# Two plain column tiles instead of four, and five groups instead of four, in the second FFN of a hybrid encoder block

## The chip, the cores and the metric

The kernel runs on one core of one Trainium2 chip. The metric is the device time of one execution in microseconds (us); lower is better. TensorE is called PE in the rows of the profile, its weight loads PEld, VectorE DVE, ScalarE ACT, GpSimd POOL, and SP is the engine that issues most DMAs.

## The reference

The block adds three things in turn to a hidden state h of 528 tokens (16 learned meta tokens and 512 real ones) by 1024 features, all in float32:

```python
h = h + 0.5 * swiglu(rms_norm(h, ffn1_norm), ffn1_w_gate, ffn1_w_up, ffn1_w_down)
u = rms_norm(h, mix_norm)
z = u @ w_in            # HGRN2 (bidirectional gated recurrence) and axial GQA from slices of z
h = h + mixed @ w_out   # mixed: both branches, gated
h = h + 0.5 * swiglu(rms_norm(h, ffn2_norm), ffn2_w_gate, ffn2_w_up, ffn2_w_down)
return h[:, N_META:]

def swiglu(x, w_gate, w_up, w_down):
    return (silu(x @ w_gate) * (x @ w_up)) @ w_down
```

The width of both FFNs is 2816, which is 22 column tiles of 128.

## The kernel before

Everything is held with features on the 128 partitions and tokens along the free dimension. The hidden state h is eight tiles of 128 x 528. The first FFN works on all 528 tokens, the second on the 512 real ones.

**Split operands.** A float32 product is made of three matmuls of a narrower type: each operand is split into a high part (a cast on ScalarE, line 84 for weights) and the rest (a subtraction on DVE, line 85), and high x high, high x rest and rest x high are summed in PSUM. `Weights` reads a list of blocks (the plan): for each block a DMA from SP into one of two `raw` buffers, then the split into `whi` and `wlo` (two buffers each); at most two blocks are prepared ahead of the one in use.

**Plain column tiles.** For the first four column tiles of an FFN (`GROUPS` and `PLAIN`), gate and up are each one `group`: 8 blocks of the contraction x 3 matmuls of 512 columns (in the first FFN 256 and 272). The normalisation's gain is folded into the operand `xt` (buffers `xh`, `xl`), and its factor R = 1/rms is applied to the results: DVE multiplies gate and up by R, ScalarE applies silu, DVE multiplies both, and the hidden tile is split into `hh` and `hl` (lines 449, 450, 452, 453, 272 and 273).

**Pairs of column tiles.** The other 18 column tiles are taken two at a time, with seven products of half size instead of eight (Winograd's form of Strassen's scheme). Contraction, tokens and columns are each cut in two; sums and differences of the four quarters of the input are multiplied by sums and differences of the four quarters of the weights. `pair` runs, for gate and for up, the products P1 (input part b11), P2 (b21), P5 (n1), P6 (n2), P7 (t3), P3 (b22) and P4 (t4), each of 4 x 3 matmuls of 256 columns (264 in the first FFN), 14 products in all. Weight sums are made by `Weights.seven` on DVE and GpSimd, and are split like other blocks: two "first", two "sums", two "more", one "last" block for a pair, in that order.

**Input parts.** `normal` prepares the input parts. `early(kk)`, for each of four kk, normalises two tiles of h into `xn` (line 331), makes n1 and n2 in `xm` (lines 335 to 337) and splits b11, b21, n1 and n2. The plain loop calls it once behind each of the four column tiles. `late()`, behind the plain tiles, makes t3, b22 and t4 (lines 351 to 353) and splits them. Its results lie in the same buffers `xh` and `xl` that the plain products read as `xt`:

```python
room = [sp.tile([P, 4, 4, nh], F32R, name=m, tag=m) for m in ("xh", "xl")]
for i, nm in enumerate(("t3", "b22", "t4")):
    parts_of[nm] = tuple(r[:, i] for r in room)
```

`xm` has a single buffer, in `early` and in `late`.

**Groups.** Behind the column tiles of each group (4, 6, 6 and 6 of them) stand the products with W_down: for each of the eight feature tiles c one weight block of 128 x (128 x group size) and 3 matmuls of 512 columns for each hidden tile; DVE then adds half of the result to h (line 468). Behind the last group's addition the second FFN stores the tile; the last feature tile is done in two halves.

**Order.** Outside the mixing stage in the middle (whose matmuls are in an order written out in the program) the instructions of an engine are ordered by a planner, by their place in the program and by when their operands are expected; the engines wait for each other through semaphores.

Of the kernel before, what the change touches and what calls it, by code (L numbers as in the profile page):

```python
# [11 lines left out]
ALU = mybir.AluOpType  # L12
# [6 lines left out]
SEQ = 512  # L19
META = 16  # L20
T = SEQ + META
# [3 lines left out]
CUT = 256  # L25
DFF = 2816
NF = DFF // P
GROUPS = ((0, 4), (4, 10), (10, 16), (16, 22))
PLAIN = 4
HEADS = 4  # L30
OFFSET = 300
EARLY = 7
# [8 lines left out]
C_FFN1, C_MIX, C_FFN2, C_LBF, C_LBB, C_ON = 0, 8, 16, 24, 32, 40  # L41
# [142 lines left out]
def block_kernel(tc, xT, wg1, wu1, wd1, w_in, wup, wout, wg2, wu2, wd2, params,  # L184
                 cosT, sinT, masks, ident_in, out):
    nc = tc.nc
    act, dve, pe, pool = nc.scalar, nc.vector, nc.tensor, nc.gpsimd

    def group(outs, w, xs, tick=None):
        hi, lo = w  # L190
        n = len(xs)
        for k in range(n):
            sl = slice(k * P, (k + 1) * P)
            xh, xl = xs[k]
            for i, (a, b) in enumerate(((hi, xh), (hi, xl), (lo, xh))):
                for o, cols in outs:
                    pe.matmul(o, a[:, sl], b[:, cols], start=(k == 0 and i == 0),  # L197
                              stop=(k == n - 1 and i == 2))
            if tick:
                tick(0.65 if len(outs) == 1 else 0.68)  # L200

    with (tc.tile_pool(name="persist", bufs=1) as sp, tc.tile_pool(name="wts", bufs=1) as wp,
          tc.tile_pool(name="psum", bufs=1, space=PSUM) as pp):
        W = Weights(nc, wp, 2)

        def ffn_plan(wg, wu, wd):
            plan = []
            for a, b in GROUPS:
                if b <= PLAIN:
                    for j in range(a, b):  # L210
                        plan += [wg[j], wu[j]]
                else:
                    for j in range(a, b, 2):
                        plan += W.seven([wg[j], wg[j + 1], wu[j], wu[j + 1]])
                plan += [wd[c][:, a * P:b * P] for c in range(KT)]
            return plan
# [32 lines left out]
        def parts(n):  # L249

            nonlocal turn
            turn += 1
            if n == SEQ:
                return [(bank(("mm", "mm", "mm", "at", "am")[turn % 5]), slice(0, SEQ))]
            if turn % 3 == 0:
                t = wide("S")
                return [(t[:, 512 - CUT:512], FULL[0]), (t[:, 512:512 + T - CUT], FULL[1])]
            return [(bank(g)[:, :c.stop - c.start], c) for g, c in zip((("mm", "mm"), ("at", "am"))[turn % 3 - 1], FULL)]
# [12 lines left out]
        def split(dst, src, cols=slice(0, T)):  # L271
            act.copy(dst[0][:, cols], src[:, cols])
            dve.tensor_tensor(dst[1][:, cols], src[:, cols], dst[0][:, cols].bitcast(F32), ALU.subtract)
# [32 lines left out]
        def normal(ft, xt, gain, n):  # L306


            nh = n // 2
            E, F = slice(0, nh), slice(nh, n)  # L310
            xn = ft.tile([P, KT, n], F32, name="xn", tag="xn")
            parts_of = {}

            def new(name, pool_t, tags):
                parts_of[name] = tuple(pool_t(t) for t in tags)

            def unit(t):
                return ft.tile([P, 4, nh], F32R, name=t, tag=t)

            def both(name, kk, src):  # L320
                hi, lo = (t[:, kk, :] for t in parts_of[name])
                act.copy(hi, src)
                dve.tensor_tensor(lo, src, hi.bitcast(F32), ALU.subtract)

            def early(kk):

                if not kk:
                    for nm in ("b11", "b21", "n1", "n2"):
                        new(nm, unit, (nm + "h", nm + "l"))
                for k in (kk, kk + 4):  # L330
                    dve.scalar_tensor_tensor(xn[:, k], h[k][:, :n], par[:, gain + k:gain + k + 1], R[:, :n],
                                             ALU.mult, ALU.mult)
                u, v = xn[:, kk], xn[:, kk + 4]
                t = ft.tile([P, 2, nh], F32, name="xm", tag="xm", bufs=1)
                dve.tensor_tensor(t[:, 0], u[:, E], u[:, F], ALU.subtract)
                dve.tensor_tensor(t[:, 1], t[:, 0], v[:, F], ALU.add)
                dve.tensor_scalar(t[:, 1], t[:, 1], -1.0, None, ALU.mult)
                both("b11", kk, u[:, E])
                both("b21", kk, v[:, E])
                both("n1", kk, t[:, 0])  # L340
                both("n2", kk, t[:, 1])

            def late():
# [4 lines that stand above are left out]
                for kk in range(4):  # L348
                    u, v = xn[:, kk], xn[:, kk + 4]
                    t = ft.tile([P, 2, nh], F32, name="xm", tag="xm", bufs=1)  # L350
                    dve.tensor_tensor(t[:, 0], v[:, F], u[:, F], ALU.subtract)
                    dve.tensor_tensor(t[:, 1], t[:, 0], u[:, E], ALU.add)
                    dve.tensor_tensor(t[:, 1], t[:, 1], v[:, E], ALU.subtract)
                    both("t3", kk, t[:, 0])
                    both("b22", kk, v[:, F])
                    both("t4", kk, t[:, 1])

            return parts_of, early, late

        def pair(ft, xq, n):  # L360
# [69 lines left out]
                step(i, w, i, "P4")  # L430
            return tiles[1]

        def ffn(ft, xt, gain, n, last):
            def hidden(u):
                hh, hl = (ft.tile([P, TP if n == T else SEQ], F32R, name=m, tag=m, bufs=7)[:, :n] for m in ("hh", "hl"))
                split((hh, hl), u, slice(0, n))
                return hh, hl

            xq, early, late = normal(ft, xt, gain, n)
            for a, b in GROUPS:  # L440
                h1 = []
                for j in range(a, b) if b <= PLAIN else ():
                    pg = parts(n)
                    group(pg, W.next(), xt)
                    pu = parts(n)
                    group(pu, W.next(), xt)
                    g, u = (ft.tile([P, TP], F32, name=t, tag=t, bufs=3)[:, :T] for t in ("g", "u"))
                    for o, c in pg:
                        dve.tensor_tensor(g[:, c], o, R[:, c], ALU.mult)
                    act.activation(g[:, :n], g[:, :n], AF.Silu)  # L450
                    for o, c in pu:
                        dve.tensor_tensor(u[:, c], o, R[:, c], ALU.mult)
                    dve.tensor_tensor(u[:, :n], u[:, :n], g[:, :n], ALU.mult)
                    h1.append(hidden(u))
                    early(j)
                if b <= PLAIN:
                    late()
                for j in range(a, b, 2) if b > PLAIN else ():
                    for u in pair(ft, xq, n):
                        h1.append(hidden(u))  # L460
                for c in range(KT):
                    w = W.next()
                    ends = b == NF and n == SEQ and c == KT - 1
                    for po in ([[(bank(g)[:, :256], slice(i, i + 256))] for g, i in (("at", 0), ("am", 256))]
                               if ends else [parts(n)]):
                        group(po, w, h1)
                        for o, cols in po:
                            dve.scalar_tensor_tensor(h[c][:, cols], o, 0.5, h[c][:, cols], ALU.mult, ALU.add)  # L468
                        if ends:
                            last(c, po[0][1])  # L470
                    if b == NF and not ends:
                        last(c)

        with tc.tile_pool(name="f1", bufs=1) as ft:
            xt = xtiles()
            W.extra = ft
            plan = ffn_plan(wg1, wu1, wd1)
            plan.insert(14, masks)
            W.plan(plan)
            dummy = ft.tile([P, 32], F32, name="dummy", tag="dummy")  # L480
# [15 lines left out]
            for k in range(KT):  # L496
                a = sums[k % 2]
# [20 lines left out]
            plan = [w_in[c] for c in order]  # L518
# [2 lines left out]
            for c in range(KT):  # L521
                plan += [w_in[Z_GA + c], wup[c][:, :512]]
            plan += [wout[c] for c in range(KT)]
            W.plan(plan + ffn_plan(wg2, wu2, wd2))
            ffn(ft, xt, C_FFN1, T, last1)


        with tc.tile_pool(name="mix", bufs=1) as mp, tc.manual_schedule(engines={pe.engine}):
# [54 lines left out]
            with tc.tile_pool(name="heads", bufs=1) as hp, tc.tile_pool(name="small", bufs=1) as mn:  # L583
# [415 lines left out]
                for c in range(KT):  # L999
# [3 lines left out]
                    b = branch(YB)  # L1003
# [5 lines left out]
            with tc.tile_pool(name="tail", bufs=1) as hp:  # L1009
# [10 lines left out]
                for c in range(KT):  # L1020
                    sg = tmp()[:, :SEQ]
                    gate(sg)
                    b = branch(YA)
# [3 lines left out]
                xt2 = xtiles(SEQ)  # L1027
                for c in range(KT):
                    b = bank("mm")
# [6 lines left out]
        with tc.tile_pool(name="f2", bufs=1) as ft:  # L1036
            W.extra = ft

            def last2(c, cols=slice(0, SEQ)):
                nc.sync.dma_start(out=out[c * P:(c + 1) * P, cols], in_=h[c][:, cols])  # L1040

            ffn(ft, xt2, C_FFN2, SEQ, last2)


def _constants():
# [59 lines left out]
```

## Time and profile before

| | |
|---|---|
| Median of 3 runs | 1206.66 us (1203.74 to 1207.83) |
| The profiled execution | 1206.21 us |
| Its span, first to last instruction | 1204.4 us |
| Mean granted clock of TensorE | 0.991 |
| Busy: PE, PEld, DVE, ACT, POOL | 1172.3, 1074.0, 879.4, 554.2, 195.2 us |

The span is cut from one execution; times in the rows count from its start. Matmuls are pipelined, so that a busy PE isn't one at its peak; weight loads run beside them. Busy times of neighbouring instructions on an engine overlap a little.

### The profile page before, as it was taken

How to read it: one execution, taken by the hardware profiler on the slowest of the kernel's cores; microseconds unless marked ns; L12 is line 12 of the kernel's file. 1: busy time of each engine (PE TensorE's matmuls, PEld its weight loads, DVE VectorE, ACT ScalarE, POOL GpSimd, SP SyncE). 2: the span in 40 equal slices, each digit the busy share in tenths (PEclk: the TensorE clock that was granted, in tenths of full speed). 3: DMA queues.
4: the chain of work that ended last, by engine and by line, in shares of the span. 5: the costliest groups of instructions: out<-in, count | busy, mean ns of one | idle time of the engine just before them, and what ended most of it. 6: DMA issues, size and time to landing. Idle time of an engine off the chain costs nothing.

```text
span 1204.4 us, 19449 instructions
## 1 busy us (share of the span) xinstructions
PE 1172.3 (97%) x7765; PEld 1074.0 (89%) x7765; DVE 879.4 (73%) x1440; ACT 554.2 (46%) x920; POOL 195.2 (16%) x158
## 2 busy tenths in 40 slices
PE   8999999999999998989999999999999999999998
PEld 8999999999999787868888788888888998998997
DVE  7988758848956788798698845454788856866863
ACT  5545425524545464545336533334444533543541
POOL 1012001001102023242132410122101101101100
PEclk9999999999999998999899999999999999999999
DMA  6133223232223210101011112233423332333213
GB/s 232 63 104 132 88 88 106 97 97 96 72 66 120 74 68 35 54 28 60 36 54 36 54 53 103 91 105 105 142 68 110 114 101 97 106 101 103 95 53 122
DMA packets 34234, 106.22 MB, mean 88 GB/s; under 512 B 3936, under 2 KB 4320, under 8 KB 34144
## 3 DMA queue, kind: packets, MB, share of 16 engines
q1 hardware_dynamic: 33984, 104.44, 26.0%
q8 instruction: 61, 1.00, 0.3%
q0 software_dynamic: 160, 0.54, 0.1%
q14 instruction: 29, 0.24, 0.1%
HBM read 102.87 MB, written 2.10 MB: 87 GB/s over the span
## 4 chain that ended last, share of the span: by engine, by line
PE 85%; DVE 10%; issue 2%; ACT 2%; DMA 0%; POOL 0%; SPq 0%; ACTq 0%; DVEq 0%; POOLq 0%
PE mm L197 34%; PE mm L374 14%; PE at L374 9%; PE at L197 5%; PE am L197 5%; PE gs L374 4%; PE S L197 4%; PE am L374 2%; PE gs L884 2%; DVE wlo L85 2%; PE mm L938 1%; PE mm L732 1%; PE S L694 1%; PE at L717 1%; ACT whi L84 1%
## 5 line engine op out<-in xcount | busy, mean ns | idle before, releaser
L84 ACT CAST whi<-raw 128x1024 fp32r<-128x1024 f32 (+2 forms) x220 | 189.5, 862 | 286.6 <-PE mm L197 123.8
L85 DVE TENSOR_TENSOR wlo<-raw,whi 128x1024 fp32r<-128x1024 f32 (+2 forms) x220 | 223.5, 1018 | 24.9 <-ACT whi L84 20.1
L197 PE MATMUL mm<-xh,whi 128*128 128x512 f32 (+1 forms) x504 | 166.8, 364 | 9.9 <-DVE tm L543 2.3
L197 PE MATMUL mm<-xl,whi 128*128 128x512 f32 (+1 forms) x504 | 160.0, 351 | 0.4 <-DVE xl L279 0.3
L197 PE MATMUL mm<-xh,wlo 128*128 128x512 f32 (+1 forms) x504 | 159.2, 349 | 0.3 <-DVE wlo L85 0.3
L116 POOL TENSOR_TENSOR sums<-raw 128x512 f32<-128x512 f32 x36 | 59.0, 1639 | 492.4 <-DVE wlo L85 492.4
L197 PEld LDWEIGHTS mm<-xh,whi 128*128 128x128 f32 x504 | 89.8, 191 | 23.2 <-DVE tm L543 2.7
L85 DVE TENSOR_TENSOR wlo<-sums,whi 128x1024 fp32r<-128x1024 f32 x72 | 87.6, 1218 | 24.9 <-ACT whi L84 24.7
L84 ACT CAST whi<-sums 128x1024 fp32r<-128x1024 f32 x72 | 75.4, 1051 | 62.6 <-DVE sums L111 21.0
L197 PEld LDWEIGHTS mm<-xh,wlo 128*128 128x128 f32 x504 | 89.1, 190 | 13.4 <-DVE wlo L85 0.8
L197 PEld LDWEIGHTS mm<-xl,whi 128*128 128x128 f32 x504 | 89.8, 192 | 10.4 <-DVE xl L279 0.9
L871 POOL TENSOR_TENSOR Z<-Z,tot 128x512 f32<-128x512 f32 x32 | 48.0, 1499 | 154.4 <-PE gs L884 129.3
L197 PE MATMUL mm<-hh,whi 128*128 128x256 f32 (+1 forms) x218 | 62.9, 333 | 0.1
L197 PE MATMUL mm<-hh,wlo 128*128 128x256 f32 (+1 forms) x218 | 63.0, 334 | 0.0
L197 PE MATMUL mm<-hl,whi 128*128 128x256 f32 (+1 forms) x218 | 62.9, 332 | 0.0
L374 PE MATMUL mm<-xl,whi 128*128 128x264 f32 (+1 forms) x216 | 61.3, 284 | 0.0
L374 PE MATMUL mm<-xh,whi 128*128 128x264 f32 (+1 forms) x216 | 61.2, 283 | 0.0
L374 PE MATMUL mm<-xh,wlo 128*128 128x264 f32 (+1 forms) x216 | 61.2, 283 | 0.0
L468 DVE SCALAR_TENSOR_TENSOR h<-mm,h 128x512 f32<-128x512 f32 (+2 forms) x40 | 21.0, 545 | 41.5 <-PE mm L197 41.3
L702 ACT ACTIVATE pr<-S,nm,yq 128x528 f32<-128x528 f32 x32 | 25.4, 794 | 38.0 <-DVE nm L699 33.7
L884 PE MATMUL gs<-Z,ks 128*128 128x128 f32 x224 | 33.7, 296 | 9.0 <-DVE A L888 3.6
L884 PEld LDWEIGHTS gs<-Z,ks 128*128 128x128 f32 x224 | 30.6, 198 | 12.8 <-issue 7.3
(367 smaller groups left out, 3418.4 us busy)
## 6 DMA issues: line engine op xcount, KB each, us to landing
raw<-in_wg SPq DMA_DIRECT2D x43, 512.0 KB, 3.3
raw<-in_wu SPq DMA_DIRECT2D x43, 512.0 KB, 3.2
raw<-in_w_in SPq DMA_DIRECT2D x42, 512.0 KB, 3.2
raw<-in_wd SPq DMA_DIRECT2D x48, 384.0 KB, 3.1
raw<-in_wd SPq DMA_DIRECT2D x16, 256.0 KB, 2.6
raw<-in_wup SPq DMA_DIRECT2D x16, 256.0 KB, 2.6
raw<-in_wout SPq DMA_DIRECT2D x8, 512.0 KB, 3.3
h<-in_xT SPq DMA_DIRECT2D x4, 528.0 KB, 6.5
```

Of the source, the lines that this page charges most:

```text
L84: nc.scalar.copy(hi[:, c], src)
L85: nc.vector.tensor_tensor(lo[:, c], src, hi[:, c].bitcast(F32), ALU.subtract)
L116: nc.gpsimd.tensor_tensor(t[:, E], r0[:, E], r1[:, E], ALU.add)
L197: pe.matmul(o, a[:, sl], b[:, cols], start=(k == 0 and i == 0), stop=(k == n - 1 and i == 2))
L374: pe.matmul(o, a[:, sl], b[:, kk, :], start=(start and kk == 0 and i == 0), stop=(kk == 3 and i == 2), skip_group_check=True)
L468: dve.scalar_tensor_tensor(h[c][:, cols], o, 0.5, h[c][:, cols], ALU.mult, ALU.add)
L694: pe.matmul(s[:, WIDE][:, cols], st[e][:, c * P:(c + 1) * P], kk[:, cols], start=(i == 0), stop=(i == 1))
L702: act.activation(pr, s[:, WIDE], AF.Exp, bias=nm, scale=r, accum_out=sm)
L717: pe.transpose(o[:, k, :], pr[:, k * P:(k + 1) * P], ident)
L732: pe.matmul(av, v[:, k, :], p[:, k, :], start=(k == 0 and i == 0), stop=False)
L871: pool.tensor_tensor(xx, xx, first, ALU.mult)
L884: pe.matmul(s[:, c, :], ks[:, c * P:(c + 1) * P], ap(Z, T + c * P, ((2 * m, P // (2 * m)), (T + m, 2), (1, m))), start=True, stop=True)
```

## The change

The second FFN gets groups of its own: 2, 6, 6, 4 and 4 column tiles, of which the first two are plain, so that ten pairs stand where nine stood and two plain tiles where four stood. The first FFN keeps 4, 6, 6 and 6. With two plain tiles, `early` is called twice behind each. In both FFNs, n2 is made by one scalar_tensor_tensor, behind the split of n1, instead of a tensor_tensor and a tensor_scalar.

```diff
-GROUPS = ((0, 4), (4, 10), (10, 16), (16, 22))
-PLAIN = 4
+GROUPS1 = ((0, 4), (4, 10), (10, 16), (16, 22))
+GROUPS2 = ((0, 2), (2, 8), (8, 14), (14, 18), (18, 22))
...
-        def ffn_plan(wg, wu, wd):
+        def ffn_plan(wg, wu, wd, groups):
             plan = []
-            for a, b in GROUPS:
-                if b <= PLAIN:
+            for a, b in groups:
+                if not a:
                     for j in range(a, b):
                         plan += [wg[j], wu[j]]
...
                 dve.tensor_tensor(t[:, 0], u[:, E], u[:, F], ALU.subtract)
-                dve.tensor_tensor(t[:, 1], t[:, 0], v[:, F], ALU.add)
-                dve.tensor_scalar(t[:, 1], t[:, 1], -1.0, None, ALU.mult)
                 both("b11", kk, u[:, E])
                 both("b21", kk, v[:, E])
                 both("n1", kk, t[:, 0])
+                dve.scalar_tensor_tensor(t[:, 1], t[:, 0], -1.0, v[:, F], ALU.mult, ALU.subtract)
                 both("n2", kk, t[:, 1])
...
-            for a, b in GROUPS:
+            for a, b in groups:
                 h1 = []
-                for j in range(a, b) if b <= PLAIN else ():
+                for j in () if a else range(b):
...
-                    early(j)
-                if b <= PLAIN:
+                    for kk in range(4 * j // b, 4 * (j + 1) // b):
+                        early(kk)
+                if not a:
                     late()
-                for j in range(a, b, 2) if b > PLAIN else ():
+                for j in range(a, b, 2) if a else ():
...
-            plan = ffn_plan(wg1, wu1, wd1)
+            plan = ffn_plan(wg1, wu1, wd1, GROUPS1)
...
-            W.plan(plan + ffn_plan(wg2, wu2, wd2))
-            ffn(ft, xt, C_FFN1, T, last1)
+            W.plan(plan + ffn_plan(wg2, wu2, wd2, GROUPS2))
+            ffn(ft, xt, C_FFN1, T, GROUPS1, last1)
...
-            ffn(ft, xt2, C_FFN2, SEQ, last2)
+            ffn(ft, xt2, C_FFN2, SEQ, GROUPS2, last2)
```

## Rows read from the trace of the kernel before

**Rows 1.** The page: the chain that ended last, by engine.

```profile
PE 85%; DVE 10%; issue 2%; ACT 2%; DMA 0%; POOL 0%; SPq 0%; ACTq 0%; DVEq 0%; POOLq 0%
```

**Rows 2.** Stretches of the second FFN: busy us (instructions), granted clock, DMA share, GB/s.

```profile
core 0: us, PE busy (x) PEld busy (x) DVE busy (x) ACT busy (x) POOL busy (x), PEclk, DMA share, GB/s
852.17:896.88 44.71, 44.71 (x196) 36.51 (x195) 38.33 (x66) 20.83 (x36) 0.00 (x0) 1.00 0.33 112
896.88:922.96 26.08, 25.90 (x122) 20.60 (x121) 23.44 (x44) 12.23 (x24) 1.30 (x1) 1.00 0.30 91
922.96:943.30 20.34, 20.34 (x168) 20.24 (x169) 18.66 (x27) 12.43 (x21) 3.72 (x3) 1.00 0.38 131
...
1013.50:1074.40 60.90, 60.90 (x505) 60.62 (x505) 51.52 (x72) 33.74 (x56) 9.20 (x5) 1.00 0.33 106
...
1168.00:1204.40 36.40, 33.04 (x162) 27.65 (x161) 12.41 (x18) 5.67 (x7) 0.00 (x0) 0.99 0.35 113
```

**Rows 3.** TensorE's timeline in the second FFN: start us, duration us, instruction.

```profile
874.95 0.39 PE L197 MATMUL mm<-xh,whi 128*128 128x512 f32 x1
...
896.71 0.39 PE L197 MATMUL am<-hh,whi 128*128 128x512 f32 x1
...
919.61 0.28 PE L374 MATMUL mm<-b11h,whi 128*128 128x256 f32 x1
```

**Rows 4.** The chain in order of time: start us, us, matmuls and their count.

```profile
864.23 5.44 PE at L197 x24
...
1016.37 1.66 PE at L374 x12
...
1022.35 1.44 PE gs L374 x12
...
1086.67 4.08 PE at L197 x18
```

**Rows 5.** DVE's timeline in the second FFN; in brackets idle us before, and releaser.

```profile
862.05 0.68 DVE L449 TENSOR_TENSOR g<-mm,R 128x512 f32<-128x512 f32 x1
862.64 1.41 DVE L331 SCALAR_TENSOR_TENSOR xn<-h,par,R 128x512 f32<-128x512 f32 x2
863.97 0.42 DVE L335 TENSOR_TENSOR xm<-xn 128x256 f32<-128x256 f32 x1
...
865.84 1.22 DVE L85 TENSOR_TENSOR wlo<-raw,whi 128x1024 fp32r<-128x1024 f32 x1
866.98 0.68 DVE L273 TENSOR_TENSOR hl<-u,hh 128x512 fp32r<-128x512 f32 x1
867.58 0.28 DVE L337 TENSOR_SCALAR xm<-xm 128x256 f32<-128x256 f32 x1
867.78 0.42 DVE L323 TENSOR_TENSOR b11l<-xn,b11h 128x256 fp32r<-128x256 f32 x1
868.12 0.42 DVE L323 TENSOR_TENSOR b21l<-xn,b21h 128x256 fp32r<-128x256 f32 x1
...
896.91 0.69 DVE L452 TENSOR_TENSOR u<-at,R 128x512 f32<-128x512 f32 x1 [3.85 <-PE at L197]
...
903.97 0.69 DVE L468 SCALAR_TENSOR_TENSOR h<-am,h 128x512 f32<-128x512 f32 x1
...
910.00 0.43 DVE L323 TENSOR_TENSOR xl<-xm,xh 128x256 fp32r<-128x256 f32 x1 [0.26 <-ACT xh L322]
```

**Rows 6.** DVE's timeline in the first pair of the second FFN.

```profile
936.92 0.42 DVE L397 SCALAR_TENSOR_TENSOR u<-u,g 128x256 f32<-128x256 f32 x1
```

**Rows 7.** The page, DMA issues: engine, count, KB each, median us to landing.

```profile
raw<-in_wd SPq DMA_DIRECT2D x16, 256.0 KB, 2.6
```

**Rows 8.** TensorE's timeline in the mixing stage; in brackets idle us before.

```profile
573.14 1.22 PE L938 MATMUL mm<-vt,A 128*128 128x128 f32 x4 [3.08 <-DVE st L927]
```

**Rows 9.** A stretch of the mixing stage, TensorE alone: busy us, clock, DMA share, GB/s.

```profile
570.00:580.00 10.00, 6.92 (x37) 0.66 0.00 0
```

**Rows 10.** A stretch of the first FFN, behind its plain tiles, TensorE alone.

```profile
65.00:70.00 5.00, 4.68 (x37) 1.00 0.20 56
```

**Rows 11.** DVE's timeline at the end of the last pair.

```profile
1169.19 0.69 DVE L273 TENSOR_TENSOR hl<-u,hh 128x512 fp32r<-128x512 f32 x1 [0.69 <-ACT hh L272]
```

More of the change, by code (lines that the diff above doesn't have):

```diff
@@ L431, in pair, with ffn @@
             return tiles[1]
-        def ffn(ft, xt, gain, n, last):
+        def ffn(ft, xt, gain, n, groups, last):
             def hidden(u):
```

## The prediction

> **What bounds the kernel now.** I read the page first: the chain that ended last is TensorE for 85% and VectorE (DVE) for 10% [rows 1], so as a whole the matmuls bind. The second FFN is then cut into stretches [rows 2]. TensorE is busy from end to end in each but the tail; DVE fills 38.33 of the 44.71 us of the plain tiles, 23.44 of the 26.08 us behind them and 18.66 of the first pair's 20.34 us. So DVE is nearly a second bound in just the stretch that the change shortens.
>
> TensorE's timeline gives the dates [rows 3]: the plain tiles start at 852.17 (where the first stretch of rows 2 is cut), the third of them at 874.95, the products with W_down at 896.71, the first pair's product P1 (b11) at 919.61 us. The chain in order of time gives prices [rows 4]: 24 plain matmuls of 512 columns take 5.44 us (227 ns each), 12 of a pair's 256 columns 1.44 us (120 ns), 18 of the down products 4.08 us (227 ns). The 96 down matmuls of the first group should take 96 x 0.227 = 21.8 us; from 896.71 to 919.61 are 22.9, so only 1.1 us are lost there today.
>
> DVE's timeline says why so little [rows 5]. With R ready, DVE is free at 862.05 and works without a break up to a wait of 3.85 us, which the last plain product ends at 896.91. late() can't be finished before that: its tiles t3, b22, t4 lie in the buffers xh and xl that the plain products read. So it runs behind the plain tiles, under 21.8 us of down products.
>
> **The change part by part.** *TensorE.* Two plain tiles go: 4 x 5.44 = 21.8 us. One pair comes: three pairs took 60.90 us [rows 2], 20.3 each. Saved: 1.5 us. The down products stay 22 x 3 x 8 matmuls in all.
>
> By the Trainium skill (TensorE: Matmul & The Clock Gate, Back-to-back issue gap) a sustained stream spaces 512-column matmuls 131 ns apart and 128-column ones 81; an estimate between them for 256 columns is 98 ns, so two plain tiles would take 96 x 131 ns = 12.6 us and a pair 168 x 98 ns = 16.4 us, and the sum below would be 5.3 us higher. The trace disagrees: 227 and 120 ns [rows 4].
>
> *DVE at the transition.* I price an instruction by the distance to the next start in a run without idle time, since neighbours overlap [rows 5]: 0.60 us for a 512-column tensor_tensor or addition into h, 0.335 for 256 columns, 0.665 for xn, 1.14 for a 1024-column weight split, 0.20 for the tensor_scalar of 256. A 256-column scalar_tensor_tensor lasts 0.42 us [rows 6] like the tensor_tensor at 868.12, so 0.34. The split of a 256-column W_down block isn't in the trace: it lies between 0.335 (the same subtraction on 256 columns) and 0.60 (on 512); I take 0.335, the row of its size. The work from 862.05 until product P7 (t3) of the first pair may start:
> evictions and splits of two plain tiles, 8 x 0.60 = 4.8; one more plain weight block, 1.1; early() for four kk, now within two tiles instead of four, 8 x 0.665 + 4 x 0.335 + 4 x 0.34 + 16 x 0.335 = 13.4; late(), 24 x 0.335 = 8.0; W_down, 8 x 0.335 + 8 additions x 0.60 = 7.5; the pair's weights: two first blocks (1.14), two sums (0.60 + 0.60 + 1.14), one "more" (0.60 + 1.14), and two evictions of P2 (0.335), 9.4. Sum 44.2 us, so 906.3 us.
> TensorE alone would be there at 874.95 + 48 x 0.227 + 8 x 1.44 = 897.4 us. The gap is 8.9 us.
>
> The same sum for the kernel before has two tiles (4.8), four plain blocks (4.6), 8 x 0.27 of wider W_down splits and four tensor_scalars more: 56.5 us, or 918.6, where P7 comes at about 919.61 + 8 x 1.44 = 931.1. There it has 12 us to spare. The change takes 21.8 us of plain products and 10.9 of down products from above DVE's work, and only 12.3 us of that work. That is the heart of the forecast.
>
> Order can't remove this debt, since what is deferred is due a little later. With the best order (t4 and b22 behind P7), the gap is 3.6 us at P7, but at P4, 5.76 us on, DVE owes these, the second "more", the last block and P7's evictions: 7.2; at the second pair's P1 about as much. So 7.2 is the low end. The high end is the order in which early() and late(), with the second tile's end 14.6 us, go before any further W_down block: TensorE stands until 889.5, then come eight blocks of 1.65 us, since two raw buffers at up to 2.6 us from issue to landing [rows 7] plus cast and split give no more, then 11.5 us to P7: 914.2, a gap of 16.8. The present trace mixes the kinds (an addition into h at 903.97 while late() runs on to 910.00 [rows 5]), so I take the sum's 8.9 plus 0.6 for waits on ScalarE like the 0.26 at 910.00: 9.5 us. The 1.1 us lost now are within it.
>
> Behind the instructions that are late on DVE stand W_down's splits and additions, without which TensorE gets neither weights nor a free bank, then the pair's weights. ScalarE casts beside every split, but is busy for only about half of these stretches [rows 2]. SP issues four 512 KB loads for the pair, as for the two tiles, and eight more of W_down, 40 for 32 with the same bytes in all; they hide behind the debt, and cost the 1.65 us a block above where DVE isn't late.
>
> *The clock.* The down products of the first two blocks last 2.7 us; then TensorE may stand for several us while DVE works off early(). After a hole of 3.08 us that ended at 573.14 [rows 8], the granted clock averages 0.66 over ten us [rows 9]: 6.8 us at 1.2 GHz, 3.4 us lost. The bounds here are nothing and 3.4; about half would fall into time that waits for DVE anyway: I take 1.5.
>
> *early() itself.* One instruction of 0.335 and one of 0.20 become one of 0.34, four times in each FFN; in the second that is in the sum. In the first TensorE is busy for only 4.68 of 5 us behind the plain tiles [rows 10]: 0 to 0.8 us come back, I take 0.4, near what is missing there.
>
> *Group sizes.* The fifth group's eight additions into h are in the sum, as the first is the one that is short of time. At a pair's end the last hidden tile is split at 1169.19 + 0.69, and its chain began 0.69 + 0.42 us ahead of that row (ScalarE's cast, P4's eviction) [rows 11]: 1.8 us. Groups of four cover that with two tiles of two blocks, 12 x 0.227 = 2.7 us: nothing; up to 1.8 us a group, were only one block at hand. Last addition and store don't change.
>
> Sum: 9.5 - 1.1 - 1.5 - 0.4 + 1.5 = +8.0 us. The profiled execution took 1206.21 us (span 1204.4), 0.45 below the median of 1206.66: **1214 us**. From the ends: 7.2 - 1.1 - 1.5 - 0.8 = +3.8 (1210.0) and 16.8 - 1.1 - 1.5 + 3.4 = +17.6 (1223.8).
>
> **The rivals.**
> *Serial order*: early() and late() go ahead of all else, TensorE stands in one long hole and resumes at half clock: 1219 to 1224. For it: they come first in the program. Against it: the mixing in rows 5. 0.13.
> *The middle of the kernel is reordered, and the result isn't slower.* The first FFN's stream of instructions is shorter, and the order planned behind it may come out otherwise. The hole before 573.14 and its clock cost 3.08 + 3.4 = 6.5 us [rows 8, 9]; if its release comes 3 us earlier, +8.0 becomes +1.5: 1208. It decides from a hole too short to move the clock. Against it: nothing in that stage is edited. 0.11.
> *The debt is hidden*, so that only matmuls count: -1.5 - 0.4, or 1204 to 1205. It decides from a gap under 3 us, and would follow if far less of DVE's work were due before P4 than I count; my best order still leaves 7.2. 0.06.
> *A pair no cheaper than two tiles*: if its 14 products went at the slowest pace seen, 1.66 us for 12 [rows 4], it would take 23.2 us, 1.4 more than the tiles; +10.9, 1217. For it: weight loads fill a pair (20.24 of 20.34 us [rows 2]). Against it: 1.44 is the rule. The skill's spacing, above, points the same way. 0.02.
> The forecast, 1210 to 1218, has 0.68.
>
> **How the numbers follow.** 0.3% (3.6 us) is about what a measurement of this kernel can tell from no change. Faster comes from the hidden debt, 0.05; the same, from the reordered middle and the rest of the hidden debt, 0.12; slower from the forecast, the serial order and the dear pair, 0.83. The range 1208 to 1221 holds the forecast, the dear pair, the upper half of the reordered middle and the lower part of the serial order; 2 in 10 at most stay outside.
>
> **What would show it.** In the profile after: plain products of FFN2 end some 22.8 us after their start; down products take 17 to 24 us instead of 10.9; DVE has hardly any idle time from R until P7; P7 starts 52 to 57 us after the plain start (45.2 without waits); pairs take 20.3 us again; groups of four start without a hole; perhaps a stretch at half clock. It is wrong if DVE idles there while TensorE waits (then an order or a load is the cause), if the first pair starts within 35 us of the plain start (the debt was hidden), or if the time moved before 850 us.

## The result, and the profile after

The changed kernel took 1216.07 us (median of 6 runs, 1214.06 to 1218.3) where the kernel before took 1206.4 us (6 runs, 1203.74 to 1207.83). The ratio is 1.0092, with a 95% interval of 1.0073 to 1.011: slower, by 0.7 to 1.1%. The forecast was 1214 us, with a range from 1208 to 1221. The two profiled spans differ by 8.9 us.

The profiled execution took 1215.04 us, its span is 1213.3 us. These are stretches of its second FFN: plain tiles, down products of the first group, first pair, a later group of six's down products, the three pairs behind them, and the last group with the tail (columns as in [rows 2]).

```profile
core 0: us, PE busy (x) PEld busy (x) DVE busy (x) ACT busy (x) POOL busy (x), PEclk, DMA share, GB/s
849.28:872.04 22.76, 22.76 (x99) 18.31 (x98) 20.43 (x33) 11.76 (x21) 0.00 (x0) 1.00 0.32 111
872.04:894.04 22.00, 15.52 (x50) 10.14 (x48) 22.00 (x56) 10.94 (x28) 0.00 (x0) 0.84 0.23 70
894.04:915.14 21.10, 20.58 (x168) 20.36 (x169) 20.46 (x25) 12.28 (x19) 5.08 (x3) 1.00 0.30 110
956.75:989.59 32.84, 32.84 (x146) 26.95 (x146) 16.29 (x21) 8.20 (x10) 1.29 (x1) 1.00 0.31 93
989.59:1050.48 60.89, 60.89 (x506) 60.61 (x505) 51.51 (x72) 33.74 (x56) 9.20 (x5) 1.00 0.32 107
1187.05:1213.30 26.25, 22.04 (x108) 18.46 (x107) 10.40 (x17) 4.36 (x7) 0.00 (x0) 0.98 0.39 130
```

The second row holds most of the story: behind the plain tiles TensorE is busy for 15.52 of 22.00 us, and DVE for all 22.00. The stretch of [rows 2] at this place also takes in the first 3.35 us of the pair; cut at P1 like the row above, the kernel before had TensorE at 22.79 of 22.90 us and DVE at 20.09:

```profile
896.71:919.61 22.90, 22.79 (x97) 17.70 (x96) 20.09 (x41) 10.97 (x22) 0.00 (x0) 1.00 0.34 103
```

The three pairs of the next group are what they were: 60.89 us, against 60.90.

TensorE's timeline of the changed kernel, the instructions with which the waits end (in brackets the idle time before, and who ended it):

```profile
872.04 0.39 PE L197 MATMUL mm<-hh,whi 128*128 128x512 f32 x1
...
874.61 0.73 PE L197 MATMUL mm<-hh,whi 128*128 128x512 f32 x2 [0.75 <-ACT hh L272]
...
877.41 0.40 PE L197 MATMUL at<-hl,whi 128*128 128x512 f32 x1
882.26 0.80 PE L197 MATMUL mm<-hh,wlo 128*128 128x512 f32 x1 [4.45 <-DVE wlo L85]
...
894.04 0.39 PE L373 MATMUL mm<-b11h,whi 128*128 128x256 f32 x1 [0.88 <-ACT whi L84]
...
906.44 0.28 PE L373 MATMUL mm<-xh,whi 128*128 128x256 f32 x1
...
1086.82 0.39 PE L373 MATMUL at<-b11h,whi 128*128 128x256 f32 x1 [0.68 <-DVE h L468]
```

Down products start at 872.04, P1 of the first pair at 894.04 and P7 (its operand t3 lies in xh) at 906.44, where [rows 3] had 896.71 and 919.61. The 48 down matmuls would take 10.9 us; they and the waits between them take 22.0. The longest wait, 4.45 us, is for the split of a W_down block. DVE's timeline shows what stood ahead of that block:

```profile
859.14 0.68 DVE L448 TENSOR_TENSOR g<-mm,R 128x512 f32<-128x512 f32 x1
...
879.76 0.43 DVE L350 TENSOR_TENSOR xm<-xn 128x256 f32<-128x256 f32 x1
...
881.78 0.43 DVE L85 TENSOR_TENSOR wlo<-raw,whi 128x256 fp32r<-128x256 f32 x1
882.11 0.43 DVE L323 TENSOR_TENSOR xl<-xm,xh 128x256 fp32r<-128x256 f32 x1
882.45 0.69 DVE L468 SCALAR_TENSOR_TENSOR h<-mm,h 128x512 f32<-128x512 f32 x1
...
892.41 0.43 DVE L323 TENSOR_TENSOR xl<-xm,xh 128x256 fp32r<-128x256 f32 x1
892.74 1.30 DVE L468 SCALAR_TENSOR_TENSOR h<-mm,h 128x512 f32<-128x512 f32 x2
894.01 1.23 DVE L85 TENSOR_TENSOR wlo<-raw,whi 128x1024 fp32r<-128x1024 f32 x1
...
901.91 3.16 DVE L117 TENSOR_TENSOR sums<-sums,raw 128x512 f32<-128x512 f32 x2
```

From 859.14 (R ready and one weight split done, 862.05 in [rows 5]) to 894.01, the split of the first pair's first block, DVE has no idle time. late()'s last split (892.41) stands ahead of the last two additions into h, which end at 894.04, as the pair starts. The wait of 0.88 us that ends there is for something else, though: the pair's first block. SP could issue its load only when DVE had split a W_down block (889.20 to 889.63) and so freed a `raw` buffer; ScalarE's cast began 3.3 us later and ended at 893.98:

```profile
889.20 0.43 DVE L85 TENSOR_TENSOR wlo<-raw,whi 128x256 fp32r<-128x256 f32 x1
```

```profile
889.66 0.33 SPq L96 DMA_DIRECT2D raw<-in_wg x1
```

```profile
892.94 1.04 ACT L84 CAST whi<-raw 128x1024 fp32r<-128x1024 f32 x1 [0.93 <-PE mm L197]
```

So DVE sets this date too, but by way of a split 4.4 us ahead of it and a load. (The profile puts the cast's wait down to TensorE; the load, issued at 889.66, took 3.2 us.) The split of a 256-column block, which the trace before didn't show, takes 0.335 us (881.78 to 882.11).

To compare kernels I count from the matmul with ones ahead of R (L302; 855.82 us before, 852.91 after), which drops what happens earlier, to the start of DVE's last addition into h (1201.08 and 1209.13), which drops the last store: it landed 3.3 to 4.2 us later from execution to execution, 4.17 and 3.39 us in two kernels that end with the same order of instructions. The FFN so counted took 345.26 us before and 356.22 us after: +10.96.

### The profile page after: what moved, and what is told of

Read it like the earlier page. It is cut to its first block, busy times and chain, and to the rows that moved or that the text cites. A ratio compares the mean times of both kernels' runs of the same rounds, so it can differ in the third digit from the quotient of the medians.

```text
span 1213.3 us, 19663 instructions
## 1 busy us (share of the span) xinstructions
PE 1170.7 (96%) x7831; PEld 1072.8 (88%) x7831; DVE 894.7 (74%) x1461; ACT 560.2 (46%) x939; POOL 197.3 (16%) x160
## 4 chain that ended last, share of the span: by engine, by line
PE 80%; DVE 14%; issue 2%; ACT 2%; DMA 0%; POOL 0%; SPq 0%; ACTq 0%; DVEq 0%; POOLq 0%
PE mm L197 31%; PE mm L373 14%; PE at L373 9%; PE gs L373 4%; PE S L197 4%; PE am L197 4%; PE at L197 4%; DVE wlo L85 3%; PE am L373 2%; PE gs L884 2%; PE S L694 1%; PE mm L732 1%; PE mm L938 1%; ACT whi L84 1%; PE at L717 1%
## 5 line engine op out<-in xcount | busy, mean ns | idle before, releaser
L84 ACT CAST whi<-raw 128x1024 fp32r<-128x1024 f32 (+3 forms) x228 | 190.2, 835 | 285.1 <-PE mm L197 124.8
L85 DVE TENSOR_TENSOR wlo<-raw,whi 128x1024 fp32r<-128x1024 f32 (+3 forms) x228 | 224.4, 987 | 24.3 <-ACT whi L84 19.6
L197 PE MATMUL mm<-xh,whi 128*128 128x512 f32 (+1 forms) x480 | 156.8, 361 | 9.1 <-DVE tm L543 2.3
L197 PE MATMUL mm<-xl,whi 128*128 128x512 f32 (+1 forms) x480 | 149.9, 347 | 1.3 <-DVE xl L279 1.3
L197 PE MATMUL mm<-xh,wlo 128*128 128x512 f32 (+1 forms) x480 | 149.1, 346 | 0.3 <-DVE wlo L85 0.3
L373 PE MATMUL mm<-xh,whi 128*128 128x256 f32 (+1 forms) x228 | 64.7, 284 | 0.0
L373 PE MATMUL mm<-xl,whi 128*128 128x256 f32 (+1 forms) x228 | 64.7, 284 | 0.0
L373 PE MATMUL mm<-xh,wlo 128*128 128x256 f32 (+1 forms) x228 | 64.5, 283 | 0.0
L197 PEld LDWEIGHTS mm<-hh,wlo 128*128 128x128 f32 x222 | 38.3, 189 | 9.8 <-DVE wlo L85 5.9
L373 PE MATMUL at<-xh,whi 128*128 128x256 f32 (+1 forms) x152 | 44.3, 291 | 0.3 <-ACT u L391 0.3
L702 ACT ACTIVATE pr<-S,nm,yq 128x528 f32<-128x528 f32 x32 | 25.4, 793 | 39.1 <-DVE nm L699 34.8
```

What stands on the lines that cost most here:

```text
L84: nc.scalar.copy(hi[:, c], src)
L85: nc.vector.tensor_tensor(lo[:, c], src, hi[:, c].bitcast(F32), ALU.subtract)
L373: pe.matmul(o, a[:, sl], b[:, kk, :], start=(start and kk == 0 and i == 0), stop=(kk == 3 and i == 2), skip_group_check=True)
L702: act.activation(pr, s[:, WIDE], AF.Exp, bias=nm, scale=r, accum_out=sm)
```

## The experiments

All are compared with the kernel before, timed beside them on the same chip (medians of 1205.67 to 1207.92 us), so ratios can be compared between experiments, medians less so. FFN means the count just given; P1 and P7 are the starts of their first matmuls, counted from the same matmul. The diffs are against the changed kernel.

| kernel | median us | ratio to before (95%) | P1 | P7 | FFN |
|---|---|---|---|---|---|
| before | 1206.4 | | 63.79 | 75.63 | 345.26 |
| changed | 1216.07 | 1.0092 (1.0073 to 1.011) | 41.13 | 53.53 | 356.22 |
| e1 | 1204.47 | 0.9988 (0.9972 to 1.0003) | 63.80 | 75.64 | 345.31 |
| e2 | 1218.5 | 1.0097 (1.007 to 1.0125) | 42.06 | 54.46 | 357.09 |
| e3 | 1204.49 | 0.9993 (0.9976 to 1.001) | 63.80 | 75.64 | 345.51 |
| e4 | 1216.21 | 1.0079 (1.0055 to 1.0102) | 41.13 | 53.52 | 355.71 |
| e5 | 1212.43 | 1.0057 (1.0039 to 1.0076) | 37.42 | 50.48 | 353.11 |
| e6 | 1221.69 | 1.0132 (1.0107 to 1.0157) | 46.60 | 60.48 | 362.23 |
| e7 | 1208.28 | 1.0021 (1.0005 to 1.0037) | 66.78 | 78.62 | 348.24 |
| e8 | 1216.7 | 1.0084 (1.0058 to 1.0111) | 41.21 | 55.10 | 357.44 |
| e9 | 1203.73 | 0.9979 (0.9965 to 0.9992) | 63.01 | 74.90 | 344.50 |
| e10 | 1215.65 | 1.0097 (1.007 to 1.0123) | 38.41 | 51.57 | 357.68 |
| e11 | 1212.56 | 1.0055 (1.0037 to 1.0072) | 41.19 | 53.57 | 354.02 |
| e12 | 1200.16 | 0.9942 (0.9921 to 0.9963) | 62.98 | 74.49 | 343.66 |

**e1, early()'s edit alone**

```diff
-GROUPS2 = ((0, 2), (2, 8), (8, 14), (14, 18), (18, 22))
+GROUPS2 = GROUPS1
```

> The changed kernel with the second FFN's groups put back to 4, 6, 6, 6: only early()'s edit is left, in both FFNs. Debt theory (the loss is DVE's work at the transition of the second FFN): the loss is gone, 1205.5 to 1206.5 us, 0 to 0.8 us below the kernel before; R of the second FFN ready 0.4 us sooner apart from the clock in the middle. Rival that the edit itself harms (n2 behind n1's split): 1208 us or more.

1204.47 us, and the second FFN is that of the kernel before to 0.05 us. The whole loss came with the groups. What early()'s edit gives back in the first FFN isn't shown. Counted from its own first matmul with ones (L302, at 22 to 24 us) to the one behind its last addition, the first FFN took 357.05 and 358.54 us in the two kernels without the edit (before, e2), and 356.92 to 358.19 in the nine that differ from them in that FFN by the edit alone; this scatter is larger than the 0.4 us looked for. The interval of the ratio holds 1.

**e2, the groups alone**

```diff
-                dve.scalar_tensor_tensor(t[:, 1], t[:, 0], -1.0, v[:, F], ALU.mult, ALU.subtract)
+                dve.tensor_tensor(t[:, 1], t[:, 0], v[:, F], ALU.add)
+                dve.tensor_scalar(t[:, 1], t[:, 1], -1.0, None, ALU.mult)
```

(both placed again ahead of the splits of b11, b21 and n1)

> The changed kernel with early()'s old tensor_tensor and tensor_scalar: only the groups change. Debt theory: 4 x 0.2 us more on DVE in the second FFN and 0.4 us lost again in the first, 1216.1 + 1.2 = 1217 us. Rival that the time hangs on the order of early() rather than on the sum of DVE's work: off by more than 2 us either way.

P1 comes 0.93 us later and the FFN is 0.87 us longer, for 0.8 us more on DVE. With two plain tiles even 0.2 us in each of the four early() calls counts at its full price; with four (e1) it counted nothing.

**e3, five groups with four plain tiles**

```diff
-GROUPS2 = ((0, 2), (2, 8), (8, 14), (14, 18), (18, 22))
+GROUPS2 = ((0, 4), (4, 10), (10, 14), (14, 18), (18, 22))
```

> The changed kernel with groups 4, 6, 4, 4, 4 in the second FFN: four plain tiles and nine pairs as before, but five groups and a last group of four. Debt theory: the fifth group's eight additions into h now stand where DVE has time, so it costs 0 to 1 us: 1206 to 1207 us; the last store lands about 0.8 us later behind the last addition, as in the changed kernel. Rival that the fifth group and its W_down blocks carry the loss: 1211 us or more.

The FFN is 0.20 us longer than in e1. A fifth group costs next to nothing where DVE has time. The last store landed 3.72 us behind the last addition's start, 3.34 in e1, but that differs from execution to execution (above), so the part of the expectation about the store isn't shown.

**e4, the small groups first**

```diff
-GROUPS2 = ((0, 2), (2, 8), (8, 14), (14, 18), (18, 22))
+GROUPS2 = ((0, 2), (2, 6), (6, 10), (10, 16), (16, 22))
```

> The changed kernel with groups 2, 4, 4, 6, 6 instead of 2, 6, 6, 4, 4: the same work, two plain tiles, the small groups early and the last group of six. Debt theory: the transition is as it was, 1215 to 1217 us, with the last store landing 0.8 us sooner behind the last addition. Rival that the first pairs repay the debt over a long group: 1218 us or more, since the second down products come after two pairs instead of three.

P1 and P7 stay to 0.01 us, the FFN is 0.5 us shorter. The transition doesn't care what follows; the rival is gone.

**e5 and e6, late()'s subtractions taken from DVE, and doubled**

```diff
-                dve.tensor_tensor(lo, src, hi.bitcast(F32), ALU.subtract)
+                if n == SEQ and name in ("t3", "b22", "t4"):
+                    act.copy(lo, src)
+                else:
+                    dve.tensor_tensor(lo, src, hi.bitcast(F32), ALU.subtract)
```

(the rests of t3, b22 and t4 are left out here: their low parts become copies of the values, so the result isn't the block's, and only the time counts)

> The changed kernel with the twelve subtractions in late() of the second FFN replaced by casts on ScalarE: the low parts of t3, b22 and t4 are copies of the values, not the rests. 12 x 0.335 = 4.0 us leave DVE at the transition and 12 x 0.31 = 3.7 us come to ScalarE, which is idle for half of it. Debt theory: P7 of the first pair starts about 4 us sooner behind the plain start (53 instead of 57.2 us), 1212 us. Rival, order and clock: the hole of 4.45 us behind the first two W_down blocks stays with its half clock, less than 1 us gained.

```diff
                 dve.tensor_tensor(lo, src, hi.bitcast(F32), ALU.subtract)
+                if n == SEQ and name in ("t3", "b22", "t4"):
+                    dve.tensor_tensor(lo, src, hi.bitcast(F32), ALU.subtract)
```

> The changed kernel with the twelve subtractions in late() of the second FFN done twice on DVE, 4.0 us more of its work at the transition, the values unchanged. Debt theory: all of it is on the path, P7 61 us behind the plain start, 1220 us. Rival, order and clock: the added work fills waits, under 1.5 us more.

4.0 us less on DVE bring P1 forward by 3.71 us and P7 by 3.05, and the FFN is 3.11 us shorter. 4.0 us more delay P1 by 5.47 us and P7 by 6.95, more than expected, and lengthen the FFN by 6.01. So DVE's work is on the path, and where it is added it costs half as much again as its own length. The trace shows where the rest arises:

```profile
896.06 0.41 DVE L85 TENSOR_TENSOR wlo<-raw,whi 128x256 fp32r<-128x256 f32 x1
```

```profile
899.90 1.04 ACT L84 CAST whi<-raw 128x1024 fp32r<-128x1024 f32 x1 [3.40 <-DMA raw<-in_wg]
```

```profile
901.00:915.00 14.00, 13.47 (x98) 0.88 0.25 80
```

The W_down split that lets the pair's first load start ends 42.07 us behind the matmul with ones, where the changed kernel has 36.72: 5.35 us later, and P1 follows it, although DVE's last addition ends only 4.29 us later (899.82 us, ahead of P1 at 901.00). From 901 to 915 us (the last row, TensorE alone) the granted clock is then 0.88 on average, where the changed kernel has 1.00 between P1 and P7; from P1 to P7 it took 13.88 us instead of 12.40.

**e7, the same doubling with four plain tiles** (the edit of e6 with the groups of e1)

> The same doubling of late()'s twelve subtractions, with four plain tiles and groups 4, 6, 6, 6 in the second FFN. By my sum DVE has some 12 us to spare there: 0 to 1.5 us above the same kernel without the doubling, 1206 to 1207.5 us. If DVE's work were on the path in that kernel too: 4 us more, 1210 us.

This one went against me: the FFN grew by 2.93 us over e1, not by 0 to 1.5. TensorE's timeline has the reason, a wait that e1 doesn't have:

```profile
907.08 0.50 PE L197 MATMUL mm<-hh,wlo 128*128 128x512 f32 x1 [2.61 <-DVE wlo L85]
```

late() stands ahead of a W_down split with four plain tiles too. DVE had time in the sum, but not at that point.

**e8, the hole filled**

```diff
-EARLY = 7
+EARLY, FILL = 7, 32
...
+                    if n == SEQ:
+                        fill = bank("gs")
+                        for _ in range(FILL):
+                            pe.matmul(fill[:, :P], ones, ones, start=True, stop=True)
```

(behind late())

> The changed kernel with 32 idle float32 matmuls of 128 columns (some 6 us, their result unused) behind the plain tiles of the second FFN, so that TensorE's hole of 4.45 us is broken up. Clock theory: without the half clock the down products are done sooner and P1 starts 1.5 to 3 us sooner, 1213 to 1214.5 us. Debt theory: DVE sets the dates, the granted clock stays at 1.00 there and the time at 1215 to 1217 us.

Rows of TensorE alone: the changed kernel where its clock fell, then e8 behind its fill and behind P1.

```profile
882.00:887.00 5.00, 4.74 (x11) 0.50 0.20 54
```

```profile
883.00:897.50 14.50, 12.19 (x47) 1.00 0.30 100
897.50:900.00 2.50, 1.98 (x11) 0.82 0.14 54
900.00:905.00 5.00, 5.00 (x34) 0.75 0.00 0
```

In the changed kernel the granted clock is 0.50 (1.2 GHz) behind the wait of 4.45 us. With the fill it stays at 1.00 (2.4 GHz) up to P1, and P1 starts at 41.21 instead of 41.13 us, although the fill (7.3 us) makes the down products start 7.1 us later. The half clock under the down products was there and cost nothing at P1, since DVE set that date. But e8 has a half clock too, only later: behind P1 (897.50) the granted clock falls to 0.82 and 0.75, where TensorE binds, P7 comes 1.57 us later than in the changed kernel, and the FFN is 1.22 us longer.

**e9 and e10, late() spread over the down products**

```diff
-            def late():
+            def late(kk):
...
-                for kk in range(4):
...
-                if not a:
-                    late()
...
+                    if not a and c % 2:
+                        late(c // 2)
```

e9 has this with four plain tiles (groups of e1), e10 with two.

> Four plain tiles and groups 4, 6, 6, 6 in both FFNs, with early()'s edit, and late() placed in four pieces behind the down products of c = 1, 3, 5 and 7 instead of ahead of them all: the same work in another order. The doubling of late()'s subtractions cost 2.9 us in the kernel with four plain tiles, where the sum of DVE's work left room; so the order theory is that late() holds up W_down's splits there too: 1.1 to 1.5 us less in the second FFN (P7 74.2 to 74.5 us behind the matmul with ones, instead of 75.6) and up to 1 us in the first, 1202.5 to 1203.5 us. Sum theory: nothing gained, 1204 to 1205 us.

> The changed kernel with late() in four pieces behind the down products of c = 1, 3, 5 and 7, as in the run before: same work, W_down's splits and additions first. Sum theory (DVE has no idle time, so its total sets the date of P7 whatever the order): P1 3 to 4 us sooner, but P7 within 0.7 us of 53.5 us behind the matmul with ones, 1215 to 1217 us. Order theory: the hole of 4.45 us and what follows from it is gone, P7 3 us sooner or more, 1213 us or less.

With four plain tiles the order was worth 0.81 us in the second FFN, less than expected, and more in the first: counted as in e1, that took 355.95 us in e9 and 355.86 in e10, 1.0 us below the lowest of the nine kernels without it. With two plain tiles P1 came 2.72 us sooner, and what the new order puts off comes due in the first pair. P7's date in the table, 51.57, is that of its first matmul alone. TensorE's order differs here: 20 matmuls of P5 and P6 follow that one (n1 and n2, for up), and P7 goes on at 904.79, 54.18 us behind the matmul with ones:

```profile
902.18 0.38 PE L374 MATMUL mm<-xh,whi 128*128 128x256 f32 x1 [0.58 <-ACT g L389]
902.41 0.28 PE L374 MATMUL gs<-n1h,wlo 128*128 128x256 f32 x1
...
904.67 0.28 PE L374 MATMUL at<-n2h,wlo 128*128 128x256 f32 x1
904.79 0.28 PE L374 MATMUL mm<-xh,whi 128*128 128x256 f32 x1
```

So the products ahead of P7 end 0.65 us later than in the changed kernel, not sooner, which is what the sum theory said of that date; the second pair is 1.37 us later (63.60 against 62.23), and the FFN 1.46 us longer. Breaking up the hole of 4.45 us gained nothing in the end.

**e11 and e12, GpSimd's sums of weights on DVE**

```diff
-            nc.gpsimd.tensor_tensor(t[:, E], r0[:, E], r1[:, E], ALU.add)
+            add(t[:, E], r0[:, E], r1[:, E], ALU.add)
```

These are e12's lines, in both FFNs of e9; e11 makes the same exchange in the second FFN of the changed kernel alone.

> The changed kernel with GpSimd's sums of weights (line 116) in the second FFN done by DVE: 0.60 us more for each on DVE, but none of DVE's instructions beside a running GpSimd, where two sums of line 117 took 3.1 us instead of 1.2. Contention theory: they take 1.2 us again, and P7 starts 0.5 to 0.8 us sooner behind the matmul with ones than 53.5 us; the time stays within 1 us of 1216. Without contention: P7 0.6 to 1.2 us later.

> Four plain tiles, groups 4, 6, 6, 6, early()'s edit and late() in four pieces in both FFNs, and GpSimd's sums of weights (line 116) done by DVE in both FFNs. With two plain tiles that move gave back 2.7 us in the second FFN, nearly all of it in waits behind the first pair. If these waits belong to the debt that two plain tiles leave on DVE, little is left to gain here: 0 to 1 us, 1202.7 to 1203.7 us. If GpSimd slows DVE on the path in any case: 2 us or more in each FFN, 1200 us.

In e11 the date of P7 didn't move (53.57), which neither expectation had: the pair's weights aren't what P7 waits for. But behind it 2.2 us came back (1.0 in the first group, 1.2 after it), although DVE has 20 more instructions. DVE's sums from 890 to 1200 us, grouped by line, in the changed kernel and in e11 (count, busy us, mean ns):

```profile
L117 DVE TENSOR_TENSOR sums<-sums,raw 128x512 f32<-128x512 f32 x20 | 21.8, 1094 | 0.0
L110 DVE TENSOR_TENSOR sums<-raw 128x512 f32<-128x512 f32 x20 | 17.8, 896 | 3.2 <-DMA raw<-in_wu 3.0
```

```profile
L116 DVE TENSOR_TENSOR sums<-raw 128x512 f32<-128x512 f32 x20 | 13.7, 684 | 0.0
L117 DVE TENSOR_TENSOR sums<-sums,raw 128x512 f32<-128x512 f32 x20 | 13.7, 683 | 0.0
L110 DVE TENSOR_TENSOR sums<-raw 128x512 f32<-128x512 f32 x20 | 13.6, 686 | 1.7 <-DMA raw<-in_wu 1.6
```

The new line 116 costs DVE 13.7 us; lines 117 and 110 get 12.3 us shorter. So DVE's sum stayed about where it was, and the gain lies in when things were ready: three waits of TensorE behind P7 in the changed kernel (0.24 us at 915.78, 0.32 at 929.13, 0.68 at 1086.82) aren't in e11. Whether DVE's shorter instructions did that, or the absence of GpSimd's own addition (1.29 us or more, against 0.68 on DVE) ahead of a pair's "more" blocks, no run separates. e12 shows that the gain wasn't tied to the debt alone: counted as in e1, its first FFN takes 353.91 us, 2.04 less than e9's; its second FFN is 0.84 us shorter, between the two expectations. At 1200.16 us it is faster than both kernels, by 0.4 to 0.8% against the one before.

## Why the prediction was right

**The pair and the tiles** (-1.5). Right. Two plain tiles took 21.8 us, pairs 20.3.

**DVE's work at the transition** (sum to P7 44.2 us, gap 8.9). The parts of the sum were right, the point at which they are due was not. Up to the pair's weights my sum has 4.8 + 1.1 + 13.4 + 8.0 + 7.5 = 34.8 us; the trace has 894.01 - 859.14 = 34.9. But all of late() and W_down's splits came before P1, so the gap opened there: 894.04 against 872.04 + 10.9 = 882.9, or 11.1 us. (What TensorE waited for in the end was the load behind one of these splits and its cast, which ended 0.06 us ahead of DVE's last addition; e6 tells the two apart.) The pair's weights, 9.4 us of my sum, then ran under 11.5 us of products and added only 0.9 us. Counting at P7, I spread 44 us over a cover that part of the work never used, and got 9.5 with waits. Measured at P7: 53.53 us against 19.13 (down products start) + 10.88 + 11.52 = 41.53 without waits, 12.0 us, where the kernel before loses 75.63 - (40.89 + 21.76 + 11.52) = 1.5. So this term was +10.5 net of what was lost before, not 9.5 - 1.1 = 8.4. The 1.65 us a block in my high end took 2.6 us as the longest load; [rows 7] give it as the median.

**The clock** (+1.5). The half clock came as foretold (0.50 from 882 to 887 us), but it cost nothing at P1, as e8 shows; the 1.5 us were wrong. The hole that gave the price, 3.08 us ahead of 573.14 [rows 8], is there in the changed kernel as well, 3.07 us ahead of 571.58, and the ten us around it are at full clock:

```profile
570.00:580.00 10.00, 7.74 (x55) 1.00 0.01 2
```

Debt and clock together were forecast at 9.9 and measured at 10.5. That they agree so well is luck: the debt was 2.1 us dearer than forecast, and the 1.5 us for the clock, which cost nothing, covered most of that.

**"12 us to spare" with four plain tiles.** Wrong, as e7 shows: 4.0 us more cost 2.9. The sum left out that DVE idles for 3.85 us until the last plain product ends [rows 5], and room ahead of that point is no room behind it. late() waits for the plain products' buffers and then stands ahead of W_down's splits. e9 took part of that back.

**early() itself** (-0.4). Not shown: in the first FFN the scatter of the kernels with the edit (1.3 us, e1) is larger than the term. Within the second FFN it was worth 0.87 (e2), against 0.8 in the sum.

**Group sizes** (nothing). Nearly right: the two groups of four show no wait at their down products, e3 puts the fifth group at 0.2 us and e4 the order at 0.5. I had not foreseen the small waits in later pairs: behind P7 the FFN lost 33.06 - 31.18 = 1.9 us beyond a pair (20.3) and 48 down matmuls (10.88), among them 0.9 in the first group's pairs and the 0.68 at 1086.82. e11, which gave back 2.2, shows that GpSimd's additions were behind most of this, by one of the two ways named there. So 1.9 us that the forecast put at nothing are part of why the time came out 2 us above 1214.

The sum of the FFN: +10.5 at P7, -1.5 for the pair, +1.9 behind it, +10.9 against 10.96 in the trace. The spans differ by less, 8.9 us, since the changed kernel's second FFN began 2.9 us earlier and its last store landed 0.85 us later.

**The signs.** P7 started 57.16 us behind the plain start, just outside the 52 to 57 that I gave. And the time did move before 850 us, which I had named as a sign of being wrong: the matmul with ones ahead of R came at 852.91 us instead of 855.82. The change needn't be the reason: e1 and e5, which don't differ from the changed kernel up to there, have it at 851.85 and 857.69.

**The rivals.** The debt wasn't hidden, and a pair is no dearer than before. The serial order came about in part, early() and the first part of late() ahead of the third W_down block, but that order didn't set the total: e10, which spreads late(), starts P1 sooner and ends the first pair later. The middle shows no sign of having been reordered: its four longest waits of TensorE are there in both (3.58, 3.13, 3.08 and 2.29 us before; 3.58, 3.12, 3.07 and 2.28 after). The waits that end at 463.94 us before and at 463.49 after are equally long, and the clock behind them differs (eight matmuls in 2.05 and in 1.13 us):

```profile
463.94 2.05 PE L884 MATMUL gs<-Z,ks 128*128 128x128 f32 x8 [3.58 <-DVE A L888]
```

```profile
463.49 1.13 PE L884 MATMUL gs<-Z,ks 128*128 128x128 f32 x8 [3.58 <-DVE A L888]
```

Between the two matmuls with ones the middle took 475.55 us before, 473.05 after, 471.81 in e1 and 476.93 in e5; none of them edits it. That is why single spans of these kernels can't be compared below some 5 us.

## What to carry to other kernels

When a stretch of cover is shortened, sum the work of the engine beneath it up to each point where it is due, and look for the earliest point that its order makes binding; slack in a longer sum is no help there. Price a slower clock or a hole only where that engine sets the date: under the down products it cost nothing here, and behind P1 in e8 it cost 1.5 us. And before moving work off a busy engine, look at what the receiving engine does to it: here taking work back from GpSimd gained 2.2 us in e11's second FFN, where the change under study lost 11.

## What was not expected of the hardware

Two additions of 512 columns on DVE (line 117, operands and result in SBUF) took 3.16 us from 901.91, while GpSimd ran two of its own:

```profile
900.75 3.78 POOL L116 TENSOR_TENSOR sums<-raw 128x512 f32<-128x512 f32 x2 [52.77 <-DVE wlo L85]
```

In e11 the same line took 683 ns each on average. The Trainium skill (SBUF — State Buffer, Who interferes with whom) says that a DVE instruction with two SBUF inputs contends with a GpSimd instruction that reads SBUF; the runs agree, 1094 against 683 ns a piece in line 117, and 12.3 us over ten pairs in lines 117 and 110. I had priced these additions at 0.60 us from rows without GpSimd beside them.
